# A streaming encoder step on one core: later values and merged matmuls of two heads, the spatial product from high and low parts, free weight splits behind the due ones

## The chip, the cores and the metric

The kernel runs on one core of a Trainium2 chip. The metric is the device time of one execution in microseconds, as the median of the runs shown. One more execution is recorded by the hardware profiler; its views are what the prediction reads. Beside the engines TensorE (PE, its weight loads PEld), VectorE (DVE), ScalarE (ACT), GpSimd (POOL) and SyncE (SP) work the DMA queues that SP, ACT and POOL issue to.

## The reference

384 rows of activations (256 of a prompt, 8 times 16 of running streams) go through two layers, all in float32.

```python
# layer 0: RMSNorm, one projection to q, k, v, gate of 8 forgetting heads and 8 stick-breaking heads
s = einsum('bqhd,bkhd->bhqk', q, k) * ATTN_SCALE + (Fq - Fk)     # forgetting: F is a running sum of log gates
o = einsum('bhqk,bkhd->bqhd', softmax(where(causal, s, -inf)), v)
a = where(before, exp(log_sigmoid(z) + after), 0.0)              # stick-breaking: sums of log_sigmoid(-z)
hp = hp + concatenate([fo * silu(fz), so * silu(sz)]) @ w_out0
# layer 1: RMSNorm, projection to u, v, z (4096 each); v is layer-normalised
mixed = einsum('gts,bnsgc->bntgc', tril(w_sp), v_in_16_groups_of_256) + b_sp
hp = hp + (u * mixed * silu(z)) @ w_out1
y = rmsnorm(hp, final_g)
```

Running streams also attend to 128 cached rows each, so that keys and values of the caches are read. The new keys, values, log gates and the normalised v are outputs too.

## The kernel before, in words

**Projections.** The 384 rows are three blocks of 128 (`NT`). The transposed activations are the stationary operand, in a high and a low part (`his`, `los`); a weight tile of 128x512 is loaded by SP into `raw` (5 buffers), ScalarE rounds it to `whi` (L84) and VectorE takes the rest, `wlo` (L86); four buffers of each. `products` (L93) makes three matmuls for each weight tile and row block: high by high, high by low, low by high (L100 to L102). `dense_nat` (L105) goes through the tiles in pairs, 18 matmuls a pair, and adds up in three banks. A projection of 512 columns in 16 tiles is 144 matmuls.

**The attention of layer 0** works in four groups of four heads (`quad`, L466): groups 0 and 1 are forgetting heads, 2 and 3 stick-breaking ones. Each group projects k, q, z and v (group 0: k, v, q, z). `head` (L601) is a generator: each `next` or `send` issues one stage. `scores` (L478) makes the score matmuls in plain float32 (L626 to L632) and the softmax or its stick-breaking counterpart of two heads; the weights `pr` go to DRAM by ScalarE's queue (L667) and come back in another order by GpSimd's (L492, four loads for two heads) so that VectorE's transpose within blocks (L670) completes the transposition into `PT`. `attended` (L497) then makes the products with the values (L678 to L686), multiplies them with the gate `gz` (L689, L691), and writes them to DRAM (L504). When all four heads are through, `blocks` (L391) loads them back, and `mix_split` (L587) transposes and splits them for the output projection.

**What sets the order.** `at(g, what, kp, f)` fills a table: work `f` is issued in the projection `what` of group `g`, ahead of its weight tile `kp`. `places` (L511) has the four places of a group: scores of heads 0 and 1, scores of 2 and 3, values of 0 and 1, values of 2 and 3; `(what == "k")` means the next group. The framework's scheduler then orders each engine's instructions by its own estimate of time; `tc.issue_after(x)` holds an instruction behind `x`. Each engine's queue runs strictly in the order so made. `gains(1)` (L162, called at L356) transposes the second layer's norm gains on TensorE and copies them out of their bank (L165); the forget sums (L358 to L373) follow it there.

**Layer 1.** v is projected, normalised in place in `vt` (`normalise`, L780: L787, L788), and each of 8 chunks of 512 columns then goes as follows: the spatial weights of two groups are loaded, transposed and masked (`spatial_weights`, L829); z and u are projected to `gate`; the spatial product (L862) is a plain float32 matmul of 128x256 for each row block and group, 48 in all; gate times product (L865) is transposed by VectorE and 16 small DMAs (`turn`, L119), split into high and low parts (L872, L873), and multiplied with `w_out1` after chunks 2, 4 and 6 (`out1`, L821) and 7. Scratch has two buffers of `gate` and of `wT`, and one of `trn`.

**The last part.** The last four k-tiles of `w_out1` are kept back (`KL = 4`): their 16 weight tiles are split ahead by `last_split` (L888), some between the tiles of the last `out1` ("due" splits), the rest free; `last` (L913) then finishes one row block after the other (L921 to L923, with pieces of 512 and of 256 columns), and `norm` writes the result.

Of the kernel before, what the change touches and what calls it, by code (L numbers as in the profile page):

```python
# [8 lines left out]
F32 = mybir.dt.float32  # L9
# [28 lines left out]
def tile_hybrid_step(  # L38
# [54 lines left out]
    def products(out, his, los, ws, kp, tbs, first, last):  # L93
# [9 lines left out]
        return mm  # L103

    def dense_nat(w, k0, c0, his, los, nk=None, between=None, out=None, ks=None):  # L105


        nk = nk or len(his)
        out = out or [dbank() for _ in range(NT)]
        for kp in range(0, nk, 2) if ks is None else ks:  # L110
            behind = ()
            if between and kp in between:
                with tc.issue_after(splits[-1]), tc.issue_after(highs[-1]):
                    behind = between[kp]() or ()
            ws = [wunit(w[(k0 + k) * P:(k0 + k + 1) * P, c0:c0 + 512], 1, 512, behind=behind) for k in (kp, kp + 1)]
            products(out, his, los, ws, kp, range(NT), 0, nk - 1)
        return out
# [39 lines left out]
    with ExitStack() as l0:  # L157
# [185 lines left out]
        def forget(o):  # L343
# [11 lines left out]
            yield  # L355
            gains(1)  # L356
            b3 = bank()
# [108 lines left out]
        def quad(g):  # L466
# [11 lines left out]
            def scores(pair):  # L478

                for hh in pair:  # L480
                    hs = slice(hh * P, hh * P + P)
                    own[hh] = head(g, h0 + hh, own["k"][:, hh], lambda hs=hs: own["v"][:, :, hs], own["q"][:, hh],
                                   keys_of[4 * g + hh], lambda n=4 * g + hh: values_of[n], lambda hs=hs: own["z"][:, :, hs])
                wd = own[pair] = dram.tile([2, 6, P, P], F32, name=nm("wd"))
                for hh in pair[::-1]:
                    next(own[hh])
                for _ in range(2):
                    for j, hh in enumerate(pair):
                        own[hh].send(wd[j])
                blk = own["blk", pair] = slot(F32).rearrange("p (j x) -> p j x", j=2)  # L490
                for j in range(4):
                    G.dma_start(blk[32 * j:32 * j + 32].rearrange("p j (a d) -> p (j a) d", d=32),  # L492
                                wd[:, :, :, 32 * j:32 * j + 32].rearrange("j x (a p) d -> p (j x a) d", p=32))
# [20 lines left out]
            for i, (what, kp) in enumerate(places):  # L514
                at(g + (what == "k"), what, kp, lambda i=i: (scores, attended)[i // 2](((0, 1), (2, 3))[i % 2]))
            at(g + 1, "q", (12, 8, 8, 8)[g], lambda: mix_split())

# [83 lines left out]
        def head(g, h, kT, values, qT, kc, vc, gate):  # L601
# [67 lines left out]
            PT = lp.tile([P, 2 * T], F32, tag="PT", name=nm("PT"))  # L669
            V.transpose(out=PT, in_=blk)  # L670
            yield
            PD = PT[:, T:]
# [89 lines left out]
    with ExitStack() as l1:  # L762
# [47 lines left out]

        ghi, glo, fgs = [], [], []
        KL = 4

        def wlast(c, k):
# [14 lines left out]
        def spatial_weights(g):  # L829
# [9 lines left out]
            return wT  # L839

        for c in range(8):
            wTs = [spatial_weights(2 * c + i) for i in range(2)]
            o = dense_nat(w_in1, 0, 2 * CW + c * 512, hh_, hl_)
            gate = lp.tile([P, NT, 512], F32, tag="gate", name=nm("gate"))
            for tb in range(NT):
# [6 lines left out]
            else:  # L852

                for j in range(2):
                    fg = slot(F32)[:, :1024]
                    G.dma_start(fg, final_g[j * 1024:(j + 1) * 1024].partition_broadcast(P))
                    fgs.append(fg)
            for tb in range(NT):
                m = bank()
                for i in range(2):  # L860
                    cs = slice(c * 512 + i * 256, c * 512 + i * 256 + 256)
                    PE.matmul(m[:, i * 256:(i + 1) * 256], lhsT=wTs[i][:, tb // 2, :], rhs=vt[:, tb, cs], start=True, stop=True)  # L862
                for i in range(2):
# [6 lines left out]
            for k in range(4):  # L870
                h3 = hi[:, k, :].rearrange("p (t q) -> p t q", q=P)
                S.activation(h3, gk_[:, k], AF.Copy)  # L872
                V.tensor_tensor(out=lo[:, k, :].rearrange("p (t q) -> p t q", q=P), in0=gk_[:, k], in1=f32(h3), op=ALU.subtract)  # L873
# [5 lines left out]
        order = [(c, k) for c in range(4) for k in range(KL)]  # L879
        x = lp.tile([P, NT, 512], F32, tag="gate", name="early")  # L880
        aside = {ck: x[:, j, :] for j, ck in enumerate(order[:3])}
        for ck, raw in aside.items():
            G.dma_start(raw, wlast(*ck))
        wl = {}
# [28 lines left out]
        def last(tb, i):  # L913
# [11 lines left out]
            V.tensor_tensor(out=ht, in0=o, in1=ht, op=ALU.add)  # L925
            sq2 = lp.tile([P, NT, 512], F32, tag="gate", name=nm("sq2"))[:, 0, :]
            S.activation(sq2[:, :n], ht, AF.Square, accum_out=ssq2[:, tb, i:i + 1])
# [64 lines left out]
```

## Time and profile before

| what | value |
|---|---|
| runs | 1812.33, 1812.5, 1813.67 us; median 1812.5 |
| the profiled execution | 1815.39 us |
| its span, first to last instruction | 1813.7 us |
| granted TensorE clock, mean | 0.995 |
| busy: TensorE, VectorE, ScalarE, GpSimd | 99%, 51%, 39%, 20% |
| matmuls recorded | 8575 (a float32 one counts as two) |
| DMA | 307.63 MB, mean 170 GB/s |

The sum of a change is made against the profiled execution's own 1815.39 us and then carried over to the median, which is 2.9 us lower. Rows of the timeline give start, length, engine, line, operation and tiles; in brackets stands the idle time before it and what ended it. A row of waits gives the total, how often, and the longest. Lengths of matmuls overlap, so TensorE's pace is read from one start to the next.

### The profile page before, as it was taken

The numbers are of one execution on the slowest core, as the hardware profiler recorded it, in microseconds if no ns is written. First come the engines' busy times: TensorE is split into PE (matmuls) and PEld (weight loads), VectorE is DVE, ScalarE is ACT, GpSimd is POOL, SyncE is SP. The second block draws the span as 40 slices with busy tenths as digits, with TensorE's granted clock in tenths as the row PEclk, the third lists the DMA queues.
The fourth block names the chain that finished last, engine by engine and source line by source line (L and its number), as shares of the span: only waits on it lengthen the run. The fifth ranks groups of instructions, "written<-read, shape, count | busy, mean of one in ns | idle before, by whom it ended". The sixth has DMA issues, their size and how long they took to land. (4 is left out here: it accounts for less than half of the span.)

```text
span 1813.7 us, 24384 instructions
## 1 busy us (share of the span) xinstructions
PE 1788.8 (99%) x8575; PEld 1483.8 (82%) x8575; DVE 924.2 (51%) x1538; ACT 710.2 (39%) x1261; POOL 369.9 (20%) x544
## 2 busy tenths in 40 slices
PE   9999799999999999999999999999999999999998
PEld 8988588888888888888888888888888888888887
DVE  6337356458448455543433544554544563455366
ACT  5435236337337344433333333333333333333334
POOL 1515524313312202200300120320130210220020
PEclk9999899999999999999999999999999999999999
DMA  6868778878876877644444444454544554555553
GB/s 195 233 179 212 201 216 216 251 196 206 238 207 179 241 204 207 189 128 128 135 129 131 138 137 146 148 146 130 157 143 128 146 154 128 145 146 150 164 145 117
DMA packets 185771, 307.63 MB, mean 170 GB/s; under 512 B 22904, under 2 KB 63152, under 8 KB 185648
## 3 DMA queue, kind: packets, MB, share of 16 engines
q1 hardware_dynamic: 127696, 225.37, 42.1%
q0 software_dynamic: 25072, 63.53, 14.1%
q10 hardware_dynamic: 32880, 17.18, 3.2%
q8 instruction: 67, 1.10, 0.3%
q14 instruction: 56, 0.46, 0.1%
HBM read 269.23 MB, written 30.47 MB: 165 GB/s over the span
## 5 line engine op out<-in xcount | busy, mean ns | idle before, releaser
L86 DVE TENSOR_TENSOR wlo<-raw,whi 128x512 fp32r<-128x512 f32 x784 | 538.0, 695 | 745.1 <-ACT whi L84 744.9
L101 PE MATMUL d<-wlo,slot 128*128 128x512 f32 x2349 | 916.6, 391 | 0.2
L102 PE MATMUL d<-whi,slot 128*128 128x512 f32 x2349 | 912.0, 389 | 0.0
L84 ACT ACTIVATE whi<-raw 128x512 fp32r<-128x512 f32 x784 | 493.4, 631 | 944.9 <-PE d L102 889.3
L100 PE MATMUL d<-whi,slot 128*128 128x512 f32 x2349 | 822.9, 391 | 0.0
L100 PEld LDWEIGHTS d<-whi,slot 128*128 128x128 f32 x2349 | 440.9, 188 | 94.3 <-ACT whi L84 1.6
L101 PEld LDWEIGHTS d<-wlo,slot 128*128 128x128 f32 x2349 | 441.0, 188 | 91.7 <-DVE wlo L86 1.0
L102 PEld LDWEIGHTS d<-whi,slot 128*128 128x128 f32 x2349 | 441.0, 188 | 91.5
L126 POOL DMA_DIRECT2D gTt<-trn x128 | 78.0, 618 | 446.0 <-issue 263.9
L396 POOL DMA_DIRECT2D slot<-d x48 | 44.1, 924 | 145.9 <-DVE wlo L86 53.6
L492 POOL DMA_DIRECT2D slot<-wd x32 | 29.4, 924 | 103.4 <-DMA wd<-pr 34.6
L833 POOL DMA_DIRECT2D wr<-in_w_sp_dram x64 | 34.9, 553 | 26.2 <-DVE wT L837 25.1
L826 DVE TENSOR_TENSOR slot<-d,slot 128x512 f32<-128x512 f32 x48 | 32.0, 686 | 12.4 <-PE d L102 12.4
L783 POOL DMA_DIRECT2D slot<-in_sgu_ln_g_dram x8 | 4.5, 567 | 135.5 <-PE d L102 135.5
L455 POOL DMA_DIRECT2D kcache<-in_cache_sb_k_dram x32 | 24.9, 786 | 32.4 <-DVE KT L621 32.4
L455 POOL DMA_DIRECT2D kcache<-in_cache_fox_k_dram x32 | 25.0, 789 | 23.4 <-DVE KT L621 22.2
L709 POOL DMA_DIRECT2D blk<-h1d x12 | 11.0, 919 | 70.7 <-DMA h1d<-slot 60.4
L799 POOL DMA_DIRECT2D bcol<-in_b_sp_dram x1 | 1.2, 1176 | 116.1 <-DVE w L798 116.1
L862 PE MATMUL a<-vt,wT 128*128 128x256 f32 x96 | 24.5, 380 | 0.0
L777 POOL TENSOR_SCALAR rsv<-mvr 128x3 f32<-128x3 f32 x1 | 0.5, 540 | 113.0 <-DVE mvr L776 113.0
L774 DVE BATCH_NORM_STATS2 stats<-vt 128x6 f32<-128x512 f32 x24 | 16.3, 690 | 11.4 <-ACT vt L773 11.4
L849 DVE SCALAR_TENSOR_TENSOR gate<-d,rstd,gate 128x512 f32<-128x512 f32 x24 | 17.4, 748 | 7.3 <-PE d L102 7.3
(239 smaller groups left out, 1201.3 us busy)
## 6 DMA issues: line engine op xcount, KB each, us to landing
raw<-in_w_in_dram SPq DMA_DIRECT2D x640, 256.0 KB, 2.8
raw<-in_w_out_dram SPq DMA_DIRECT2D x189, 256.0 KB, 3.4
slot<-d POOLq DMA_DIRECT2D x48, 192.0 KB, 6.2
d<-slot ACTq DMA_DIRECT2D x24, 256.0 KB, 3.9
wd<-pr ACTq DMA_DIRECT2D x16, 384.0 KB, 5.8
slot<-wd POOLq DMA_DIRECT2D x32, 192.0 KB, 5.3
gTt<-trn POOLq DMA_DIRECT2D x128, 48.0 KB, 3.5
kcache<-in_cache_fox_k_dram POOLq DMA_DIRECT2D x32, 128.0 KB, 5.8
```

What stands on the lines that cost most here:

```text
L84: highs.append(S.activation(hi, raw, AF.Copy).ins)
L86: splits.append(V.tensor_tensor(out=lo, in0=raw, in1=f32(hi), op=ALU.subtract).ins)
L100: PE.matmul(o, lhsT=his[k][:, t], rhs=hi[:, 0, :], start=(k == first), stop=False)
L101: PE.matmul(o, lhsT=his[k][:, t], rhs=lo[:, 0, :], start=False, stop=False)
L102: mm = PE.matmul(o, lhsT=los[k][:, t], rhs=hi[:, 0, :], start=False, stop=(k == last))
L126: G.dma_start(dst[32 * j:32 * j + 32, :, 32 * a:32 * a + 32], trn[32 * a:32 * a + 32, :, 32 * j:32 * j + 32])
L396: r = G.dma_start(blk[32 * j:32 * j + 32].rearrange("p h (a d) -> p (h a) d", d=32), d[:, :, 32 * j:32 * j + 32].rearrange("h (a p) d -> p ...
L455: G.dma_start(k[32 * j:32 * j + 32].rearrange("p (b d) -> p b d", d=32), (c_fox_k, c_sb_k)[n // 8][:, :, n % 8, 32 * j:32 * j + 32].rearra ...
L492: G.dma_start(blk[32 * j:32 * j + 32].rearrange("p j (a d) -> p (j a) d", d=32), wd[:, :, :, 32 * j:32 * j + 32].rearrange("j x (a p) d -> ...
L826: evicted = V.tensor_tensor(out=h1[c][:, tb, :], in0=o[tb], in1=h1[c][:, tb, :], op=ALU.add)
L833: G.dma_start(wr[js, 0, :].rearrange("p (a s) -> p a s", s=32), w_sp[g, :, js].rearrange("(a p) s -> p a s", p=32))
L862: PE.matmul(m[:, i * 256:(i + 1) * 256], lhsT=wTs[i][:, tb // 2, :], rhs=vt[:, tb, cs], start=True, stop=True)
```

## The change

The diff, cut to its core (renamed lines and the helper's reuse of buffers follow from it):

```diff
+            last_product[:] = [products(out, his, los, ws, kp, range(NT), 0, nk - 1).ins]
...
-            gains(1)
             b3 = bank()
...
             V.tensor_copy(Fnat, b4[:, :24].rearrange("p (t h) -> p t h", h=8))
+            gains(1)
...
-                for _ in range(2):
-                    for j, hh in enumerate(pair):
-                        own[hh].send(wd[j])
+                with tc.issue_after(last_product[0]):
+                    for hh in pair:
+                        next(own[hh])
+                for j, hh in enumerate(pair):
+                    own[hh].send(wd[j])
...
-                for j, hh in ((1, pair[1]), (0, pair[0])):
-                    own[hh].send(own["blk", pair][:, j, :])
-                for hh in pair:
-                    next(own[hh])
+                turned = [own[hh].send(own["blk", pair][:, j, :]) for j, hh in ((1, pair[1]), (0, pair[0]))]
+                with tc.issue_after(turned[0].ins), tc.issue_after(turned[1].ins):
+                    for hh in pair:
+                        next(own[hh])
...
-            places = ((("z", 12), ("k", 2), ("k", 8), ("k", 12)), (("z", 12), ("v", 2), ("k", 2), ("k", 8)))[g > 0]
+            places = (((0, "z", 12), (1, "k", 2), (1, "k", 12), (1, "q", 4)), ((0, "z", 12), (0, "v", 2), (1, "k", 2), (1, "k", 8)))[g > 0]
...
-            at(g + 1, "q", (12, 8, 8, 8)[g], lambda: mix_split())
+            at(g + 1, *(("z", 4) if g == 0 else ("q", 8)), lambda: mix_split())
...
-            wT = lp.tile([P, 2, P], F32, tag="wT", name=nm("wT"))
+            wT = lp.tile([P, 2, P], F32, tag="wT", bufs=1, name=nm("wT"))
...
+            wh = lp.tile([P, 2, P], F32R, tag="wTh", name=nm("wTh"))
+            wl = lp.tile([P, 2, P], F32R, tag="wTl", name=nm("wTl"))
+            split(wh, wl, wT)
+            return wh, wl
+
+        def split_values(c):
+
+            vh = lp.tile([P, NT * 4, P], F32R, tag="trn", bufs=1, name=nm("vh")).rearrange("p (t x) q -> p t (x q)", t=NT)
+            vl = lp.tile([P, NT, 512], F32R, tag="vl", bufs=1, name=nm("vl"))
+            for tb in range(NT):
+                split(vh[:, tb, :], vl[:, tb, :], vt[:, tb, c * 512:c * 512 + 512])
+            return vh, vl
...
-                    PE.matmul(m[:, i * 256:(i + 1) * 256], lhsT=wTs[i][:, tb // 2, :], rhs=vt[:, tb, cs], start=True, stop=True)
+                    PE.matmul(o, lhsT=wh[:, tb // 2, :], rhs=vh[:, tb, cs], start=True, stop=False)
+                    PE.matmul(o, lhsT=wh[:, tb // 2, :], rhs=vl[:, tb, cs], start=False, stop=False)
+                    PE.matmul(o, lhsT=wl[:, tb // 2, :], rhs=vh[:, tb, cs], start=False, stop=True)
...
+            if c < 7:
+                vhl = split_values(c + 1)
...
-        while len(order) > 9:
-            last_split()
+        with tc.issue_after(splits[-1]), tc.issue_after(highs[-1]), tc.issue_after(turned.ins):
+            while len(order) > 9:
+                last_split()
```

In words: in group 0 the values of heads 0 and 1 move from weight tile 8 of the next group's k to tile 12, those of heads 2 and 3 from tile 12 of that k to tile 4 of its q, and mixing from tile 12 of q to tile 4 of z. In all groups the score matmuls of two heads are held behind the last projection matmul issued, and the value products of two heads behind both transposes, so that they stand together. `gains(1)` comes after the forget sums. In layer 1 the spatial weights and the normalised values are split into high and low parts, and three matmuls of fp32r take the place of one of float32; `gate` and `wT` get one buffer instead of two, and `vh` shares the buffer of `trn`. Three raw tiles of the last part go to a slot of their own instead of `gate`'s second buffer. At the end the four free splits that stood between the due ones are held behind the last due split and the transposed gate.

The order shows three places. First TensorE, around the values of heads 2 and 3 of group 0 (`d` are the banks of a projection, `whi` its weight tiles with their numbers, `PT` the transposed softmax weights). Before, with 138 projection matmuls since the same heads' last score row:

```order
L102 MATMUL d_397_2157<-whi_410_2198,slot_13_130 128x512
L678 MATMUL a_377_2033<-vnat_104_611,PT_376_2031 32x128 x4
L682 MATMUL a_377_2033<-vcache_361_1965,PT_376_2031 32x128 x8
L678 MATMUL a_378_2046<-vnat_104_611,PT_375_2029 32x128 x4
L682 MATMUL a_378_2046<-vcache_362_1967,PT_375_2029 32x128 x8
```

and now, with 214 of them:

```order
L100 MATMUL d_392_2106<-whi_428_2288,slot_16_133 128x512
L681 MATMUL a_407_2171<-vnat_104_611,PT_406_2169 32x128 x4
L685 MATMUL a_407_2171<-vcache_373_2025,PT_406_2169 32x128 x8
L681 MATMUL a_408_2184<-vnat_104_611,PT_405_2167 32x128 x4
L685 MATMUL a_408_2184<-vcache_374_2027,PT_405_2167 32x128 x8
```

The piece itself is the same; it stands 76 projection matmuls later, in q instead of k.

Second VectorE, at the two transposes that this piece needs. Before:

```order
L86 TENSOR_TENSOR wlo_408_2194<-raw_406_2190,whi_407_2192 128x512
L86 TENSOR_TENSOR wlo_411_2200<-raw_409_2196,whi_410_2198 128x512
L670 STREAM_TRANSPOSE PT_375_2029<-slot_336_1816 128x768
L670 STREAM_TRANSPOSE PT_376_2031<-slot_336_1816 128x768
L689 SCALAR_TENSOR_TENSOR gz_300_1679<-a_377_2033,st_328_1780,gz_300_1679 128x128 x2
```

and now:

```order
L86 TENSOR_TENSOR wlo_426_2284<-raw_424_2280,whi_425_2282 128x512
L86 TENSOR_TENSOR wlo_429_2290<-raw_427_2286,whi_428_2288 128x512
L674 STREAM_TRANSPOSE PT_405_2167<-slot_336_1816 128x768
L674 STREAM_TRANSPOSE PT_406_2169<-slot_336_1816 128x768
L86 TENSOR_TENSOR wlo_432_2314<-raw_430_2310,whi_431_2312 128x512
L86 TENSOR_TENSOR wlo_435_2320<-raw_433_2316,whi_434_2318 128x512
L86 TENSOR_TENSOR wlo_438_2344<-raw_436_2340,whi_437_2342 128x512
L692 SCALAR_TENSOR_TENSOR gz_300_1679<-a_407_2171,st_328_1780,gz_300_1679 128x128 x2
```

The transposes moved behind six more weight splits, and three further splits now stand between them and the multiplication with the gate.

Third VectorE in layer 1, where the transposed gate of chunk 0 is split (`gTt`), and the values of chunk 1 now too (`vl`). Before:

```order
L86 TENSOR_TENSOR wlo_1991_9819<-raw_1989_9815,whi_1990_9817 128x512
L873 TENSOR_TENSOR slot_1936_9569<-gTt_1933_9549,slot_1935_9568 128x384 x4
L86 TENSOR_TENSOR wlo_1998_9850<-raw_1996_9846,whi_1997_9848 128x512
L86 TENSOR_TENSOR wlo_2001_9856<-raw_1999_9852,whi_2000_9854 128x512
L86 TENSOR_TENSOR wlo_2004_9880<-raw_2002_9876,whi_2003_9878 128x512
L86 TENSOR_TENSOR wlo_2007_9886<-raw_2005_9882,whi_2006_9884 128x512
L787 SCALAR_TENSOR_TENSOR vt_6963<-vt_6963,mvr_6965,slot_2044_10089 128x512 x3
```

and now:

```order
L86 TENSOR_TENSOR wlo_2003_9863<-raw_2001_9859,whi_2002_9861 128x512
L898 TENSOR_TENSOR slot_1942_9597<-gTt_1939_9577,slot_1941_9596 128x384 x4
L91 TENSOR_TENSOR vl_1944_9607<-vt_6963,vh_1943_9606 128x512 x2
L790 SCALAR_TENSOR_TENSOR vt_6963<-vt_6963,mvr_6965,slot_2056_10133 128x512 x3
L91 TENSOR_TENSOR vl_1944_9607<-vt_6963,vh_1943_9606 128x512
L86 TENSOR_TENSOR wlo_2010_9894<-raw_2008_9890,whi_2009_9892 128x512
```

Three splits of values and the normalising that stood four weight splits later now stand between two weight splits.

More of the change, by code (lines that the diff above doesn't have):

```diff
@@ L508, in attended @@
                     mixed.append(blocks(own["d"])[0])
-            places = ((("z", 12), ("k", 2), ("k", 8), ("k", 12)), (("z", 12), ("v", 2), ("k", 2), ("k", 8)))[g > 0]
+            places = (((0, "z", 12), (1, "k", 2), (1, "k", 12), (1, "q", 4)), ((0, "z", 12), (0, "v", 2), (1, "k", 2), (1, "k", 8)))[g > 0]
             at(g, "q", 2 if g == 0 else 14, lambda: turned("k"))
             at(g, "z", 12, lambda: turned("q"))
-            for i, (what, kp) in enumerate(places):
-                at(g + (what == "k"), what, kp, lambda i=i: (scores, attended)[i // 2](((0, 1), (2, 3))[i % 2]))
-            at(g + 1, "q", (12, 8, 8, 8)[g], lambda: mix_split())
+            for i, (later, what, kp) in enumerate(places):
+                at(g + later, what, kp, lambda i=i: (scores, attended)[i // 2](((0, 1), (2, 3))[i % 2]))
+            at(g + 1, *(("z", 4) if g == 0 else ("q", 8)), lambda: mix_split())
             def evict(o, dst, scale, n=512):
@@ L809, in tile_hybrid_step @@
         G.affine_select(out=btri, in_=btri, pattern=[[-16, 8], [-1, 16]], compare_op=ALU.is_ge, fill=0.0, base=0, channel_multiplier=1)
-        ghi, glo, fgs = [], [], []
+        ghi, glo, fgs, aside = [], [], [], {}
         KL = 4
+        order = [(c, k) for c in range(4) for k in range(KL)]
         def wlast(c, k):
@@ L843, in tile_hybrid_step @@
             o = dense_nat(w_in1, 0, 2 * CW + c * 512, hh_, hl_)
-            gate = lp.tile([P, NT, 512], F32, tag="gate", name=nm("gate"))
+            gate = lp.tile([P, NT, 512], F32, tag="gate", bufs=1, name=nm("gate"))
             for tb in range(NT):
@@ L857, in tile_hybrid_step @@
                     fgs.append(fg)
+                x = slot(F32).rearrange("p (j c) -> p j c", j=3)
+                for j, ck in enumerate(order[:3]):
+                    aside[ck] = x[:, j, :]
+                    G.dma_start(x[:, j, :], wlast(*ck))
             for tb in range(NT):
@@ L875, in tile_hybrid_step @@
             glo.append(lo)
+            if c < 7:
+                vhl = split_values(c + 1)
             if c in (2, 4, 6):
                 out1((c - 2) * 4, 8)
[L879 to L883, printed above, removed]
         wl = {}
```

15 lines of the change are left out of this document (8 added, 7 removed).

## The prediction

> **What bounds the kernel now.** I read the page's first two parts first, to see which engine has no slack and where it stops.
>
> ```profile
> span 1813.7 us, 24384 instructions
> ...
> PE 1788.8 (99%) x8575; PEld 1483.8 (82%) x8575; DVE 924.2 (51%) x1538; ACT 710.2 (39%) x1261; POOL 369.9 (20%) x544
> ...
> PE   9999799999999999999999999999999999999998
> ...
> PEclk9999899999999999999999999999999999999999
> ```
>
> TensorE is busy in 99% of the span. A single slice, the fifth, drops to 7, and the clock drops with it. Elsewhere the time is the sum of the starts of matmuls, so a change pays only if it shortens what stands in TensorE's row or removes a stop there. Next came the list of TensorE's waits.
>
> ```profile
> PE a L678 <- DVE PT L670: 13.5, 1, 13.5
> PE a L373 <- DVE gT L165: 1.3, 1, 1.3
> PE a L196 <- DVE ones L132: 1.1, 1, 1.1
> PE a L219 <- DMA slot<-in_x_sample_dram: 0.3, 1, 0.3
> ```
>
> One wait of 13.5 us matters: the product with the values (L678) of heads 2 and 3 of the first group waits until VectorE has transposed the weights (L670). The timeline of TensorE prices it, beside the same product of the second group (320.67 on), which waits for nothing. Columns: start, length, instruction.
>
> ```profile
> 195.63 0.39 PE L102 MATMUL d<-whi,slot 128*128 128x512 f32 x1
> 209.53 0.65 PE L678 MATMUL a<-vnat,PT 128*32 128x128 f32 x8 [13.51 <-DVE PT L670]
> 214.32 0.48 PE L100 MATMUL d<-whi,slot 128*128 128x512 f32 x1
> 320.67 0.39 PE L101 MATMUL d<-wlo,slot 128*128 128x512 f32 x1
> 320.90 0.39 PE L102 MATMUL d<-whi,slot 128*128 128x512 f32 x1
> 324.03 0.47 PE L100 MATMUL d<-whi,slot 128*128 128x512 f32 x1
> ```
>
> Projection matmuls start every 0.23 us (320.67, 320.90; I count 0.227). From the last projection before the piece to the first behind it, it takes 18.69 us at 195.63 and 3.13 at 320.90: 15.56 us more, of which 13.5 are the wait. The rest is the clock, in the windows (the last three numbers are granted clock, DMA share and GB/s):
>
> ```profile
> 196.00:200.00 4.00, 0.02 (x1) 0.00 (x0) 0.00 (x0) 0.24 (x1) 0.00 (x0) 1.00 0.91 269
> 200.00:208.00 8.00, 0.00 (x0) 0.00 (x0) 0.36 (x1) 0.00 (x0) 6.41 (x8) 0.51 0.55 146
> 208.00:212.00 4.00, 2.47 (x48) 2.17 (x48) 1.48 (x2) 0.00 (x0) 0.63 (x1) 0.50 0.08 16
> ```
>
> The clock is still full through the first 4 us of idleness and is halved after it, so the piece itself runs at half clock. Who is late is read from ScalarE's, GpSimd's and VectorE's timelines and the page's table of DMA issues (last number: median us from issue to landing).
>
> ```profile
> 185.53 0.38 ACTq L667 DMA_DIRECT2D wd<-pr  x1
> 200.46 3.70 POOL L492 DMA_DIRECT2D slot<-wd  x4 [9.53 <-DMA wd<-pr]
> 207.64 1.84 DVE L670 STREAM_TRANSPOSE PT<-slot 128x768 f32<-128x768 f32 x2 [12.41 <-DMA slot<-wd]
> wd<-pr ACTq DMA_DIRECT2D x16, 384.0 KB, 5.8
> slot<-wd POOLq DMA_DIRECT2D x32, 192.0 KB, 5.3
> ```
>
> The softmax weights leave at 185.53, GpSimd gets to load them back at 200.46 (a trip of some 14 us where the median is 5.8), and VectorE starts at 207.64. It ends at 209.48. That is a chain of transfers; TensorE merely asked too early.
>
> **The change part by part.** *Later values.* The orders of before and after put 138 projection matmuls between the scores of heads 2 and 3 and their values, and now 214. The 76 more take 76 x 0.227 = 17.25 us, so TensorE asks at 195.63 + 17.25 = 212.9. If the chain ends as it did, at 209.5, the wait is gone with 3.4 us to spare, and 15.56 us with it. But the chain ran while TensorE stood and the weight stream had ebbed (DMA share 0.55). With the median of 5.3 for the last of the four loads, issued at 203.2, the transposes end at 203.2 + 5.3 + 1.8 = 210.3. If the softmax weights also leave 3 us later (their last part now stands on VectorE behind the products of heads 0 and 1), TensorE waits 0.4 us. Ends: nothing and 3 us; I take 0.3, near the first end, since both nearest rows leave it uncovered only when they add up. VectorE has the two transposes six weight splits later than before; blocked there, it holds back the next splits, which TensorE needs only behind the value piece (3 us). *Mixing* moves along with the values, still 144 projections behind them, and on VectorE eight weight splits behind the last product as in the last group, where nothing waits: nothing.
>
> *gains(1)* moves behind the forget sums. L373 waited for a bank that L165 empties; the bank it takes now was emptied long before. The 1.3 us go. They could come back as one wait for another bank: 0 to 1.3, I take the whole gain.
>
> *Merged matmuls.* The first pair of each group already had its scores in one piece (268.63 to 271.71), the second had them in five pieces with 19 projections from the first row to the last (279.78 to 287.00).
>
> ```profile
> 268.63 0.39 PE L102 MATMUL d<-whi,slot 128*128 128x512 f32 x1
> 271.71 0.50 PE L100 MATMUL d<-whi,slot 128*128 128x512 f32 x1
> 279.78 0.39 PE L102 MATMUL d<-whi,slot 128*128 128x512 f32 x1
> 287.00 0.50 PE L100 MATMUL d<-whi,slot 128*128 128x512 f32 x1
> ```
>
> One piece: 3.08 - 0.23 = 2.85. Five pieces: 7.22 - 19 x 0.227 = 2.91. Four groups save 4 x 0.06 = 0.2 us; the merged values of heads 0 and 1 I count at nothing. Merging costs nothing else: both heads' transposes are done long before.
>
> *Spatial product.* Now 48 float32 matmuls of 256 columns; then 144 of the high and low parts. The price of the first is read where four stand together, that of the second from the last part of the kernel, which has such matmuls, each with its own weight load.
>
> ```profile
> 1071.77 0.84 PE L100 MATMUL d<-whi,slot 128*128 128x512 f32 x3
> 1072.45 1.89 PE L862 MATMUL a<-vt,wT 128*128 128x256 f32 x8
> 1073.98 0.58 PE L101 MATMUL d<-wlo,slot 128*128 128x512 f32 x1
> 1074.40 0.40 PE L102 MATMUL d<-whi,slot 128*128 128x512 f32 x1
> ...
> 1788.35 0.28 PE L921 MATMUL d<-slot,slot 128*128 128x256 f32 x1
> 1788.46 0.28 PE L922 MATMUL d<-slot,slot 128*128 128x256 f32 x1
> 1788.47 0.19 PEld L923 LDWEIGHTS d<-slot,slot 128*128 128x128 f32 x1
> 1789.18 0.28 PE L922 MATMUL d<-slot,slot 128*128 128x256 f32 x1
> ```
>
> Without the four, L102 would start at 1072.45 + 0.23 = 1072.68 instead of 1074.40: 1.72 us, 0.43 each with the return to the projections; 48 x 0.43 = 20.6 us. From 1788.35 to 1789.18 seven matmuls start, 0.119 apart; 144 x 0.119 = 17.1. Gain 3.5 us. The Trainium skill (FP8 and Floating Point Precision, section TensorE Precision Notes) says that true FP32 takes four passes through the array; three reduced passes would then cost 0.75 x 0.43, the 48 products 15.5 us and the gain 5.1. The trace's 3 x 0.119 = 0.36 against 0.43 decides for 3.5.
>
> The splits for it are new: in each of eight chunks three of 128x512 and two of 128x256 on ScalarE and VectorE.
>
> ```profile
> L91 DVE TENSOR_TENSOR wlo<-raw,whi 128x512 fp32r<-128x512 f32 x16 | 10.9, 689 | 17.8 <-ACT whi L90 17.8
> 1095.38 1.95 DVE L873 TENSOR_TENSOR slot<-gTt,slot 128x384 fp32r<-128x384 f32 x4
> 1104.11 2.07 DVE L787 SCALAR_TENSOR_TENSOR vt<-vt,mvr,slot 128x512 f32<-128x512 f32 x3
> 1010.00:1690.00 680.00, 679.79 (x2999) 562.29 (x2998) 332.03 (x536) 228.66 (x373) 108.14 (x185) 1.00 0.50 145
> 1760.00:1790.00 30.00, 30.00 (x140) 25.04 (x139) 22.86 (x38) 14.85 (x31) 0.00 (x0) 1.00 0.37 114
> ```
>
> On VectorE that is 3 x 0.69 + 2 x 0.45 (between 0.34, half of the large one, and 0.69) = 3.0 us a chunk, 24 in all, beside 332 busy of 680. What hides it is VectorE's idle half, and the four buffers of each weight half. Worst is the first chunk, where the order puts 1.95 + 3 x 0.69 + 2.07 = 6.1 us between two weight splits. A pair of weights feeds 18 matmuls, 4.1 us; the buffers give two pairs less the two splits (1.4): 6.8 us. 6.1 plus the next split, 0.7, just reaches it. Ends: 0 and 4 us (half a microsecond in each chunk); I take 0.5, since seven chunks are less dense. TensorE was full in this part before, so freeing VectorE gains nothing.
>
> *Free splits behind the due ones* at the end: TensorE is busy 30.0 of 30.0 us there, so nothing is to be won. The first product of the last part needs one of the splits moved back; the transposed gate's four (1.95) and this one (0.69) fit in the 6.8 us of cover. Ends 0 and 2; I take 0.
>
> **Sum.** 15.6 + 1.3 + 0.2 + 3.5 - 0.3 - 0.5 = 19.8 us. The profiled execution took 1815.39 us with a span of 1813.7, so it becomes 1795.6; the median of the three runs, 1812.5, becomes 1792.7.
>
> **The rivals.** *A, part of the wait stays.* For it: DMA share 0.91 at 196 and a weight trip of 14 us; the weight stream no longer ebbs. Against: 3.4 us of spare. A wait of 3 to 8 us, the longer ones at half clock afterwards: 1796 to 1801. 14%.
>
> *B, the wait moves whole.* If the trip is delayed as much as the request, by the weight transfers that now go on, 15.6 us stand in place of the 0.3: 1808.0. Against it: up to the request, GpSimd's order issues the same transfers ahead of it as before. 6%.
>
> *C, weight loads bind the narrow products.* 144 loads of 0.19 us are 27.4 us where 17.1 are forecast: 10.3 us more, 1803.0. The row at 1788.47 speaks against it: the load lasts 0.19, yet matmuls start every 0.119. [...] 5%.
>
> *D, slower: VectorE becomes the bound in layer 1.* If none of the new splits is hidden, because each stands in its row between weight splits that TensorE already waits for, 8 x 3.0 = 24 us come in place of the 0.5: 1816.2. It decides against the change from 20.3 / 8 = 2.5 us a chunk. For it: only the burst at the first chunk. Against: 51% idle. 4%.
>
> **How the numbers follow.** The forecast has 71%, by itself 1790 to 1796 (lower end: no losses, 0.8, and 1.9 for a better price of the products; upper: 3 us of wait). With most of A the range is 1789.5 to 1799. A measurement of this kernel can tell about 0.2%, 3.6 us. Forecast, A, B and C are faster by more (96%); D gives 3 slower and 1 same; for a mishap in an unknown place I move 1 from faster to same: 0.95, 0.02, 0.03.
>
> **What would show it.** TensorE's waits without L678 (its new line L681) and L373, the clock 0.99 or more in the fifth slice, value pieces of about 3.1 us each. The spatial matmuls 0.12 us apart, with no stop over 0.5 us around VectorE's splits in layer 1. A wait at L681 of over 3 us, or gaps of 1 us or more in each chunk, would prove the sum wrong.

## The result, and the profile after

The kernel after takes 1795.61 us in the median of four runs (1793.76 to 1795.94), the one before 1813.09 beside it. The ratio is 0.9902, with a 95% interval of 0.9887 to 0.9916: 17.5 us less, where 19.8 were forecast. A second comparison, among the experiments, gave 1794.29 and 0.9893 (0.9878 to 0.9908), 18.9 us less.

The page of after, its span, busy times and slices:

```profile
span 1794.2 us, 24567 instructions
PE 1782.1 (99%) x8623; PEld 1480.1 (82%) x8623; DVE 946.6 (53%) x1578; ACT 729.0 (41%) x1301; POOL 369.9 (21%) x544
PE   9999999999999999999999999999999999999998
PEclk9999999999999999999999999999999999999999
```

The hole in the fifth slice is gone, and the clock's dip with it. The list of TensorE's waits in after (us in total, times, longest):

```profile
PE d L101 <- DVE wlo L86: 1.7, 3, 1.3
PE a L198 <- DVE ones L134: 1.1, 1, 1.1
PE a L886 <- DVE vl L91: 0.5, 3, 0.2
PE d L253 <- DVE slot L228: 0.4, 1, 0.4
```

The waits of 13.5 us at the values and of 1.3 at L373 are no longer there. The first row is new: 1.3 us for the low part of a weight tile, which no step of the prediction had. It is followed up below. First the piece that had waited, in TensorE's timeline of after:

```profile
209.71 0.39 PE L100 MATMUL d<-whi,slot 128*128 128x512 f32 x1
210.02 0.43 PE L681 MATMUL a<-vnat,PT 128*32 128x128 f32 x8
...
212.69 0.39 PE L689 MATMUL a<-vnat,PT 128*128 128x128 f32 x2
212.83 0.47 PE L101 MATMUL d<-wlo,slot 128*128 128x512 f32 x1
```

From projection to projection it now lasts 212.83 - 209.71 = 3.12 us, as the piece of the second group did. VectorE and GpSimd show why it no longer waits:

```profile
205.73 1.84 DVE L674 STREAM_TRANSPOSE PT<-slot 128x768 f32<-128x768 f32 x2 [0.85 <-DMA slot<-wd]
```

```profile
194.37 3.68 POOL L496 DMA_DIRECT2D slot<-wd  x4 [7.22 <-issue]
```

GpSimd loads the weights at 194.37 and VectorE has transposed them by 207.57, 2.5 us before TensorE asks (3.4 were forecast).

Now the new stop, first on TensorE and then on VectorE, both from after's timelines:

```profile
236.31 0.39 PE L100 MATMUL d<-whi,slot 128*128 128x512 f32 x1
237.99 0.50 PE L101 MATMUL d<-wlo,slot 128*128 128x512 f32 x1 [1.30 <-DVE wlo L86]
```

```profile
229.92 0.69 DVE L86 TENSOR_TENSOR wlo<-raw,whi 128x512 fp32r<-128x512 f32 x1 [2.13 <-ACT whi L84]
235.58 1.78 DVE L594 STREAM_TRANSPOSE vnat<-slot 128x1536 f32<-128x1536 f32 x1 [4.97 <-DMA slot<-d]
237.29 1.25 DVE L86 TENSOR_TENSOR wlo<-raw,whi 128x512 fp32r<-128x512 f32 x2
```

VectorE stands 4.97 us in front of the transpose for mixing (L594), whose data is not yet loaded. Behind it in its row wait the next weight splits, and TensorE waits for the first of them. The two starts on TensorE lie 1.68 us apart where 0.23 is usual.

To compare profiles stage by stage I count projection matmuls (L100 to L102), the first one as number 0: both kernels have 7191 of them, so number n starts at the same point of the work. Against the first profile of before, after is 1.52 us earlier at the first one, and from there to the last gains 17.93 us more: 1.56 up to number 135 (L373), 15.63 from number 441 to 656 (the values of heads 2 and 3), 1.57 lost from 750 to 760 (the mixing), some 0.3 by merging in four groups, and 2.08 from number 2300 to the last, which is layer 1. What lies behind the last projection takes 41.9 us in both.

### The profile page after: what moved, and what is told of

Its sections match the earlier page's. It is cut to its first block, busy times and chain, and to the rows that moved or that the text cites. A ratio compares the mean times of both kernels' runs of the same rounds, so it can differ in the third digit from the quotient of the medians.

```text
span 1794.2 us, 24567 instructions
## 1 busy us (share of the span) xinstructions
PE 1782.1 (99%) x8623; PEld 1480.1 (82%) x8623; DVE 946.6 (53%) x1578; ACT 729.0 (41%) x1301; POOL 369.9 (21%) x544
## 4 chain that ended last, share of the span: by engine, by line
PE 95%; DMA 2%; issue 1%; DVE 1%; POOL 1%; ACT 0%; POOLq 0%; DVEq 0%; ACTq 0%
PE d L100 29%; PE d L102 29%; PE d L101 29%; DMA slot<-in_sgu_ln_b_dram 1%; PE a L101 1%; PE a L100 1%; PE a L102 1%; DMA d<-gz 0%; PE a L636 0%; DMA slot<-d 0%; PE a L630 0%; PE a L886 0%; PE d L426 0%; PE a L685 0%; PE d L944 0%
## 5 line engine op out<-in xcount | busy, mean ns | idle before, releaser
L102 PE MATMUL d<-whi,slot 128*128 128x512 f32 x2349 | 911.5, 389 | 0.0
L100 PE MATMUL d<-whi,slot 128*128 128x512 f32 x2349 | 822.4, 390 | 0.0
L100 PEld LDWEIGHTS d<-whi,slot 128*128 128x128 f32 x2349 | 440.6, 188 | 93.9 <-issue 0.8
L102 PEld LDWEIGHTS d<-whi,slot 128*128 128x128 f32 x2349 | 440.9, 188 | 91.1
L830 DVE TENSOR_TENSOR slot<-d,slot 128x512 f32<-128x512 f32 x48 | 32.4, 689 | 13.8 <-PE d L102 13.8
L457 POOL DMA_DIRECT2D kcache<-in_cache_fox_k_dram x32 | 25.0, 787 | 22.1 <-DVE KT L625 20.9
L777 DVE BATCH_NORM_STATS2 stats<-vt 128x6 f32<-128x512 f32 x24 | 16.2, 689 | 11.6 <-ACT vt L776 11.6
L862 ACT ACTIVATE gate<-d,rstd 128x512 f32<-128x512 f32 x24 | 16.5, 689 | 11.2 <-PE d L102 11.1
```

The source lines that it names most:

```text
L100: PE.matmul(o, lhsT=his[k][:, t], rhs=hi[:, 0, :], start=(k == first), stop=False)
L102: mm = PE.matmul(o, lhsT=los[k][:, t], rhs=hi[:, 0, :], start=False, stop=(k == last))
L457: G.dma_start(k[32 * j:32 * j + 32].rearrange("p (b d) -> p b d", d=32), (c_fox_k, c_sb_k)[n // 8][:, :, n % 8, 32 * j:32 * j + 32].rearra ...
L830: evicted = V.tensor_tensor(out=h1[c][:, tb, :], in0=o[tb], in1=h1[c][:, tb, :], op=ALU.add)
```

## The experiments

**The kernel before once more**, without an edit.

> The kernel before, profiled a second time. In its first profile the first projection matmul starts 10.13 us into the span, after the change at 8.61: 1.52 us that no part of the change accounts for. Theory (the start varies from execution to execution): another start, between 8 and 11 us, and the same waits as in the first profile, 13 to 14 us at L678 and 1.3 at L373, total 1811 to 1816. Rival (the start belongs to the order of the kernel before): 10.1 us again, within 0.2, and the change then owns 1.5 us that the sum doesn't contain.

TensorE's waits in this second profile of before:

```profile
PE a L678 <- DVE PT L670: 13.2, 1, 13.2
PE a L196 <- DVE ones L132: 1.1, 1, 1.1
PE a L219 <- DMA slot<-in_x_sample_dram: 0.6, 1, 0.6
PE a L373 <- DVE gT L165: 0.5, 1, 0.5
```

The profiled execution took 1815.26 us. The wait at the values stands as it was; the one at L373 is 0.5 in place of 1.3. The first projection starts at 10.84. Over all thirteen profiles of this study it starts between 8.28 and 8.79 or between 9.98 and 10.84: 10.13 and 8.71 in programs with layer 0 as before, 8.61 and 10.36 in programs whose first 50 us are those of after. The 1.52 us of the start are therefore no part of the change, as the theory had it.

**The later places alone**, on the kernel before: the two lines of the table, with the loop that reads it.

```diff
-            places = ((("z", 12), ("k", 2), ("k", 8), ("k", 12)), (("z", 12), ("v", 2), ("k", 2), ("k", 8)))[g > 0]
+            places = (((0, "z", 12), (1, "k", 2), (1, "k", 12), (1, "q", 4)), ((0, "z", 12), (0, "v", 2), (1, "k", 2), (1, "k", 8)))[g > 0]
...
-            at(g + 1, "q", (12, 8, 8, 8)[g], lambda: mix_split())
+            at(g + 1, *(("z", 4) if g == 0 else ("q", 8)), lambda: mix_split())
```

> The kernel before with the later places for values and mixing alone. Theory (this place is worth 15.6 us, and the mixing behind it now costs 1.6): a wait of 13.5 us gone at L678, a new one of 1 to 2 us for a weight split behind the mixing transpose L590, and 14 us (13.3 to 15) less up to the 819th projection matmul: 1799 at the kernel before's median of 1813.1. Rival one (part of the gain needs the merged matmuls, which hold the value products behind both transposes): 11 us or less. Rival two (the new wait at the mixing comes from the merged matmuls, not from the places): 15.6 us and no such wait.

TensorE's largest wait, and VectorE's row at the mixing (L590 in this kernel):

```profile
PE d L101 <- DVE wlo L86: 3.0, 1, 3.0
```

```profile
240.21 1.78 DVE L590 STREAM_TRANSPOSE vnat<-slot 128x1536 f32<-128x1536 f32 x1 [6.71 <-DMA slot<-d]
```

The values gain 15.63 us, as much as in after, without the merged matmuls: rival one falls. So does rival two, since the stop at the mixing is here too. It is 3.30 us (by starts), twice that of after, so the program is 12.35 us ahead at projection 819, where I had expected 13.3 to 15. One execution took 1802.43, where 1799 was expected.

**The values of heads 2 and 3 put back**, in the kernel after; the mixing stays in its place in the table.

```diff
-            places = (((0, "z", 12), (1, "k", 2), (1, "k", 12), (1, "q", 4)), ((0, "z", 12), (0, "v", 2), (1, "k", 2), (1, "k", 8)))[g > 0]
+            places = (((0, "z", 12), (1, "k", 2), (1, "k", 12), (1, "k", 14)), ((0, "z", 12), (0, "v", 2), (1, "k", 2), (1, "k", 8)))[g > 0]
```

> The changed kernel with the values of heads 2 and 3 of group 0 alone put back to 138 projection matmuls behind their scores; mixing stays eight splits behind. Theory (the chain of transfers, not TensorE's request, sets when the transposes end, and the full DMA behind the request is what makes the mixing late): TensorE waits 12 to 15 us at L681, at half clock behind it, the wait of 1.3 us behind the mixing transpose is gone: 13 to 15 us more, 1809 to 1811. Rival (the changed place of heads 0 and 1 or the merged order already shortens the chain): a wait under 8 us, 1804 or less.

TensorE's waits in this kernel:

```profile
PE a L681 <- DVE PT L674: 12.2, 1, 12.2
PE a L198 <- DVE ones L134: 1.1, 1, 1.1
PE a L886 <- DVE vl L91: 0.4, 2, 0.2
```

12.2 us come back in one place (14.3 with the slower clock behind it), and the stop at the mixing is gone: 1809.24. For the values the theory held: the chain of transfers sets the time, whenever TensorE asks. For the mixing the expectation had one thing wrong: its transpose stands sixteen weight splits behind the last product of the values here and not eight, since only the values moved back. So the missing stop is no proof by itself. But the eighth split ends at 226.93, and the last load for the mixing lands at 227.95 in the trace: 1.0 us of idling at the old distance, close to the 0.63 of before, where TensorE did not stop.

What stretches the chain to the mixing is seen where the stored heads (d from gz) go out ahead of it. The windows of after around that place (the last three numbers are granted clock, DMA share, GB/s), and the issues of 213 to 229 us with their median time to landing:

```profile
212.00:220.00 8.00, 8.00 (x42) 6.75 (x41) 5.37 (x10) 1.90 (x3) 3.77 (x5) 1.00 1.03 325
220.00:228.00 8.00, 8.00 (x37) 6.63 (x36) 2.76 (x4) 4.29 (x7) 2.82 (x4) 1.00 0.97 309
```

```profile
slot<-d POOLq DMA_DIRECT2D x4, 192.0 KB, 7.0
d<-gz POOLq DMA_DIRECT2D x2, 192.0 KB, 9.1
```

The same in this experiment, the windows and the issue of 211 to 214 us:

```profile
204.00:212.00 8.00, 5.27 (x62) 4.65 (x63) 2.71 (x6) 0.00 (x0) 1.82 (x2) 0.55 0.26 72
212.00:220.00 8.00, 8.00 (x37) 6.59 (x36) 3.54 (x7) 2.62 (x5) 4.43 (x6) 1.00 0.61 197
```

```profile
d<-gz POOLq DMA_DIRECT2D x2, 192.0 KB, 3.5
```

Around TensorE's wait the weight stream ebbs (share 0.26, then 0.61), and the stores land 3.5 us after issue. Where TensorE never stands, the share is 1.03 and the same stores need 9.1. The queues show whose transfers these are, first in before (215 to 219.3 us), then in after (214.5 to 224.7), each while the stores are under way. Packets, MB and share of the DMA engines; q1 is the queue that carries the weights, 225 of 308 MB over the whole kernel, and q0 the one of GpSimd:

```profile
q0 software_dynamic: 278, 0.91, 58.8%
d<-gz POOLq DMA_DIRECT2D x2, 192.0 KB, 3.5
```

```profile
q0 software_dynamic: 703, 2.30, 61.2%
q1 hardware_dynamic: 716, 1.32, 36.8%
```

In before no weights move beside the stores, in after they take 36.8%. From the issue of the first store to the landing of the mixing's last load, the traces show 15.0 to 16.2 us in the four profiles in which TensorE stood at the values, and 19.7 to 21.6 in the nine others. The wait that the change removed had kept the way clear for the mixing. How much of the longer trip is the weights, and how much GpSimd's own loads beside them, is not separated.

**The kernel after again, and the mixing later.** These two and the last two below (scale and shift) were timed together, each in four runs, beside seven of before (median 1813.17).

> The changed kernel once more, on the chip of the versions it is compared with. Theory: 1795.6 within 1; the wait of 1.3 us for a weight split behind the mixing transpose (L594) of group 0 is there again, since full DMA stretches every such trip. Rival (a chance of that one execution): no wait there.

```diff
-            at(g + 1, *(("z", 4) if g == 0 else ("q", 8)), lambda: mix_split())
+            at(g + 1, *(("z", 8) if g == 0 else ("q", 8)), lambda: mix_split())
```

> The changed kernel with the mixing of group 0 at tile 8 of z instead of tile 4: its transpose stands three weight splits later on VectorE. Theory (VectorE stood 4.97 us in front of it while weight splits waited behind it): the wait of 1.57 us is gone, nothing new comes: 1794.0. Rival (the transfers come later too, pushed by the weights that go on): a wait of 1 us or more at another split, 1795.6. Rival on the other side (the mixed parts are then late for something behind): slower than 1795.6.

VectorE at the mixing, in the kernel after again, then with the mixing later:

```profile
233.48 1.78 DVE L594 STREAM_TRANSPOSE vnat<-slot 128x1536 f32<-128x1536 f32 x1 [2.75 <-DMA slot<-d]
```

```profile
237.04 1.78 DVE L594 STREAM_TRANSPOSE vnat<-slot 128x1536 f32<-128x1536 f32 x1 [1.79 <-DMA slot<-d]
```

After again took 1794.29 (1793.59 to 1795.94), and its profile has no stop at the mixing at all: my expectation fell, the rival (a chance of that execution) held. With the mixing later it took 1794.42 (1794.09 to 1795.50), ratio 0.9894 (0.9877 to 0.9910): no measurable difference. The stop is absent there as well, though the transpose could not start before 237.04, later than in after (235.58), where TensorE stopped: the three further weight splits cover a late chain. The median gains nothing from it; after again had no stop in its profile to lose. The profiles of all kernels that mix at the place of after, with the values behind 214 projections, give the rule. VectorE's idle time ahead of the transpose, the excess on TensorE by its starts, and the difference:

| kernel | idle us | stop us | difference |
|---|---|---|---|
| later places alone | 6.71 | 3.30 | 3.41 |
| two spatial products | 5.71 | 2.30 | 3.41 |
| three small parts undone | 4.98 | 1.57 | 3.41 |
| after | 4.97 | 1.56 | 3.41 |
| split of the values twice | 2.85 | 0 | |
| after again | 2.75 | 0 | |
| scale and shift elsewhere | 2.74 | 0 | |

There is 3.4 us of cover at this place. What exceeds it, TensorE waits, one for one, and the transpose stands behind the 69th weight split on VectorE in all seven. Whether it exceeds hangs on when the transfers land in that execution, four times in seven here.

The traces show where these executions part. GpSimd loads k back (its first four slot<-d of this stretch) ahead of the mixing, and those loads wait for three stores of k from ScalarE's queue. The third store in after and in after again, issued at 190.91 and 191.03, with the time to landing:

```profile
d<-slot ACTq DMA_DIRECT2D x1, 256.0 KB, 15.4
```

```profile
d<-slot ACTq DMA_DIRECT2D x1, 256.0 KB, 7.5
```

In the four executions that stop it takes 15.3 to 17.1 us, in the three others 7.4, 7.5 and 13.4. Where it is late, everything behind it is: GpSimd begins to load k at 206.85 in after and at 202.00 in after again, sends the second of the stored heads at 215.79 and 214.52, and has the mixing's data at 235.50 and 233.40. That is an order seen in seven profiles; no edit tried it.

**The spatial product alone**, all else as before (places, gains(1), merging, free splits).

> The changed layer 1 alone: spatial product from high and low parts with its buffers, everything else (places, gains(1), merging, free splits) as before. Theory: layer 1 is 2.1 us shorter, as in the changed kernel (3.2 by the matmuls' own starts, 1.1 given back in longer stops), layer 0 is unchanged, with 13 to 14 us of wait at the values: 1811. Rival (the record's price of the splits, 0.5): 3.0 us. Rival (four passes for float32, three for the parts): 5 us.

It took 1810.95. For layer 1 I take the time from projection 2300 to the last:

| kernel | layer 1, us |
|---|---|
| before, its two profiles | 1130.92, 1130.45 |
| later places alone | 1130.47 |
| after, its two profiles | 1128.84, 1128.68 |
| mixing later | 1128.94 |
| values of heads 2 and 3 back | 1127.67 |
| spatial product alone | 1127.39 |
| two spatial products | 1122.75 |
| split of the values twice | 1132.77 |
| scale and shift elsewhere | 1128.84 |
| that and mixing later | 1129.65 |
| three small parts undone | 1129.10 |

So the spatial product gains 3.5 us in this execution against the first profile of before (3.1 against the second), and 2.1 in after. On each engine the order of layer 1 is the same in after and in the kernel with the values put back, and yet they are 1.2 us apart. The difference lies in chunks 3, 5 and 7. Starts that come over 0.06 us later than the usual spacing (0.227 us behind a projection, 0.119 behind a spatial product), from projection 3936 on, add up to 2.4 us in after, 1.4 with the values put back and 1.0 with the spatial product alone. One such place in after, on VectorE and then on TensorE:

```profile
1650.22 0.75 DVE L791 SCALAR_TENSOR_TENSOR vt<-vt,rsv,slot 128x512 f32<-128x512 f32 x1 [0.62 <-DMA slot<-in_sgu_ln_b_dram]
...
1653.42 0.69 DVE L91 TENSOR_TENSOR vl<-vt,vh 128x512 fp32r<-128x512 f32 x1
1654.02 0.69 DVE L830 TENSOR_TENSOR slot<-d,slot 128x512 f32<-128x512 f32 x1
```

```profile
1653.71 0.28 PE L885 MATMUL a<-vh,wTh 128*128 128x256 f32 x1
1654.16 0.38 PE L886 MATMUL a<-vl,wTh 128*128 128x256 f32 x1 [0.17 <-DVE vl L91]
1654.38 0.28 PE L887 MATMUL a<-vh,wTl 128*128 128x256 f32 x1
1654.50 0.28 PE L885 MATMUL a<-vh,wTh 128*128 128x256 f32 x1
```

Normalising waits for its shift vector, the split of the values stands behind it, and the product behind that; the later products stand 0.12 us apart, as forecast. I had taken one profile's 2.1 us for the part's worth; it is 1.5 to 3.5, and the 3.0 on record lies inside.

**Two spatial products instead of three**

```diff
-                    PE.matmul(o, lhsT=wh[:, tb // 2, :], rhs=vl[:, tb, cs], start=False, stop=False)
-                    PE.matmul(o, lhsT=wl[:, tb // 2, :], rhs=vh[:, tb, cs], start=False, stop=True)
+                    PE.matmul(o, lhsT=wh[:, tb // 2, :], rhs=vl[:, tb, cs], start=False, stop=True)
```

> The changed kernel without the third of the three spatial products (low part of the weights times high part of the values): 48 matmuls of 256 columns less; this part of the computation is left out. Theory (each costs the time between two starts, 0.119 us): 5.7 us less in layer 1, 1789.9. Rival (the weight load of 0.19 us binds): 9.0 us less. Rival (a pass costs a quarter of a float32 product's 0.43 us): 5.2 us less. Rival (the products stand where TensorE waits for VectorE anyway): under 4 us less.

Layer 1 is 6.09 us shorter than in after and 5.93 shorter than in after again: 0.124 to 0.127 for each of 48 products. That is little more than their own starts (5.7), and their loads of 0.19 us don't bind (9.0 would have gone). The Trainium skill (FP8 and Floating Point Precision, section TensorE Precision Notes) counts four passes for float32; as an estimate from that, a pass would cost a quarter of the 0.43 us, 0.107. The trace doesn't agree with that as a price: the product costs 0.119 to 0.127, and 0.43 is 3.4 to 3.6 of them. This execution took 1790.35, a stop of 2.30 us at the mixing included.

**The values split twice**

```diff
-            for tb in range(NT):
-                split(vh[:, tb, :], vl[:, tb, :], vt[:, tb, c * 512:c * 512 + 512])
+            for _ in range(2):
+                for tb in range(NT):
+                    split(vh[:, tb, :], vl[:, tb, :], vt[:, tb, c * 512:c * 512 + 512])
```

> The changed kernel with the values' split done twice in each chunk: 24 more tiles of 128x512 on ScalarE and on VectorE, 0.69 us each on VectorE, 16.5 us in all. Theory (VectorE has room in layer 1 except around the products of chunks 3, 5 and 7, where the split ends last): in these three some 2 us each, elsewhere nothing: 3 to 8 us more in all, 1799 to 1804. Rival (VectorE bounds all of layer 1): 16 us or more, 1812. Rival (all is hidden, and the stops come from the loads of the normalisation alone): under 1 us more.

The first row of TensorE's waits in this kernel:

```profile
PE d L100 <- DVE slot L830: 2.7, 3, 0.9
```

Layer 1 is 3.9 us longer, for 16.5 us of VectorE's time: most of it is hidden. One execution took 1798.19. What is not stands in chunks 3, 5 and 7, where TensorE now waits for banks that VectorE adds to the residual too late. The rivals fall: VectorE doesn't bound layer 1, and its work isn't free either.

**The three small parts undone**

```diff
+            gains(1)
             b3 = bank()
...
-                with tc.issue_after(last_product[0]):
...
-                with tc.issue_after(turned[0].ins), tc.issue_after(turned[1].ins):
...
-        with tc.issue_after(splits[-1]), tc.issue_after(highs[-1]), tc.issue_after(turned.ins):
-            while len(order) > 9:
-                last_split()
+        while len(order) > 9:
+            last_split()
```

> The changed kernel with its three small parts undone: gains(1) back ahead of the forget sums, score and value matmuls no longer held together, the free splits of the last part back between the due ones. The three stand far apart, so the profile prices each. Theory: 1.3 to 1.6 us of wait at L373 comes back, the merging gives 0.06 us a group (0.2 in all), the free splits nothing (under 0.2): 1797.4. Rival for the merging (it keeps value products away from late transposes): a wait of over 1 us at one of the value pieces. Rival for the free splits: over 0.5 us behind the first product of the last part.

TensorE's waits in this kernel:

```profile
PE d L101 <- DVE wlo L86: 1.5, 2, 1.3
PE a L198 <- DVE ones L134: 1.1, 1, 1.1
PE a L375 <- DVE gT L167: 0.9, 1, 0.9
```

Against after, 1.27 us come back by projection 135 (the wait for gains(1), L375 here), as forecast, and 0.32 through the four groups, where 0.2 were. No value product waits, so the rival for the merging falls. The free splits are worth 0.3 where I had said nothing: in the last output product one split is late, as this kernel's timeline of TensorE shows.

```profile
1745.60 0.39 PE L100 MATMUL d<-whi,slot 128*128 128x512 f32 x1
1745.98 0.50 PE L101 MATMUL d<-wlo,slot 128*128 128x512 f32 x1
1746.32 0.40 PE L102 MATMUL d<-whi,slot 128*128 128x512 f32 x1
```

0.38 and 0.34 stand where 0.23 is usual. The same gap is in the kernel with the spatial product alone and in none of the three profiles with layer 1 as before: the new splits make the free ones late, and their new place mends that. One execution took 1797.52.

**Scale and shift in another buffer**, meant to free the normalising in chunks 3, 5 and 7 from waiting for a slot.

```diff
-            lg = slot(F32)[:, :1024].rearrange("p (a c) -> p a c", a=2)
+            lg = lp.tile([P, NT * 4, P], F32, tag="gTt", bufs=1, name=nm("lg"))[:, :8, :].rearrange("p (a x) q -> p a (x q)", a=2)
```

> The changed kernel with the scale and shift of the normalisation of layer 1 loaded into the buffer of the transposed gate instead of a slot: in chunks 3, 5 and 7 their loads no longer wait for a slot that an output product frees, so that normalising and splitting the values stand earlier and apart from the other work of VectorE. Theory (2.4 us of stops in layer 1 come from this crowd): 1 to 2.4 us less, 1793.2 to 1794.6. Rival (the crowd comes from the transposed gate's split and the weights alone): no change, 1795.6. Rival (a single shared buffer makes the next chunk's load wait for the gate): 1 us or more slower.

> The changed kernel with both edits: mixing at tile 8 of z, and scale and shift in the buffer of the transposed gate. Theory: the sum of the two, 2.6 to 4 us less than the changed kernel, 1791.6 to 1793. Rival: if one of the two only moves its stop, half of that or nothing.

TensorE's waits with the buffer changed alone:

```profile
PE a L198 <- DVE ones L134: 1.1, 1, 1.1
PE d L100 <- DVE slot L830: 0.9, 2, 0.6
```

The waits for the split of the values (L886) have gone, and waits for the residual's additions (L830) stand in their place. Layer 1 takes 1128.84 us, as in after, and 1129.65 with the mixing later as well. The medians are 1794.73 (1794.51 to 1795.73; ratio 0.9895, 0.9880 to 0.9910) and, with both edits, 1795.39 (1794.14 to 1796.83; 0.9898, 0.9883 to 0.9913). My theory, that the crowd around the products could be thinned, falls for this edit: it moves the stop. Nor did the edit free the normalising: VectorE now idles 12.2 us in all ahead of it (L790, seven times, up to 4.5) until its scale has landed in the shared buffer, where after has 2.6. What thinning the crowd would bring is therefore not shown. Apart from the kernel with two products, which leaves a part of the computation out, no version here is measurably faster than the kernel after.

## Why the prediction was right, and where not

*The values.* 15.6 us forecast, 15.63 found, with the places alone as well (15.2 against the second profile of before). The residual wait of 0.3 did not come: rivals A and B fell. That the chain ends earlier than TensorE asks, by 2.5 us in place of 3.4, was the step at risk, and it held by luck in part. The way back through DRAM was longer than forecast, 8.4 us for the last of the four loads in place of 5.3, and the way out shorter, 9.9 in place of the 14.2 that the prediction kept; together 22.1, against 21.6 in before.

*The mixing* is the step that failed. The prediction let it move along "still 144 projections behind" the values "where nothing waits: nothing". It had counted instructions, and the distance was indeed kept; but the trip that lies within that distance was one of the kernel before, made after TensorE had stood, with no weights moving beside the stores. With the weight stream going on, the stores take 9.1 us in place of 3.5, the transpose comes late, and TensorE stops by what exceeds 3.4 us: by 1.6 to 3.3 in four executions of seven, by nothing in three. For the values the prediction had weighed the stronger traffic; for the next chain behind them it had not.

*gains(1)*: 1.3 forecast, 1.56 found against the first profile of before. The whole wait went, but it is itself 0.5 to 1.3 from one execution to another.

*Merging*: 0.2 forecast, 0.3 found.

*Spatial product*: 3.5 less 0.5 for bursts on VectorE. The products' own starts cost what was forecast (0.119 to 0.127 each). The term for the stops was too small: 1.0 to 2.5 us in place of 0.5. They were put at the first chunk, as the worst; they came in chunks 3, 5 and 7, where the shift vector lands late. The net is 1.5 to 3.5 in these profiles. Rivals C and D fell with the two experiments on them.

*Free splits*: nothing forecast, 0.3 found, and only beside the new layer 1.

*The sum.* In after again, where the mixing doesn't stop, the part from the first projection to the last gains 19.5 us, against 19.8 on record. That nearness is luck in part: the values and gains(1) bring 0.6 more than their terms, layer 1 0.8 less, and against the second profile of before it is 18.7. In the first profile of after the gain is 17.9, with the stop of 1.6. The medians are 17.5 and 18.9 us apart, and the forecast of 1792.7 was 2.9 and 1.6 us too low. A stop of 0 to 3.3 at the mixing and a layer 1 that gains 2 rather than 3 are of that size.

What stays open: why the third store of k lands 7 us after its issue in one execution and 15 in another. The late chain to the mixing follows it in the profiles, but no experiment moved that store.

## What to carry to other kernels

A stop on the bounding engine also idles the queues that feed it. Whoever removes it must price every chain of transfers behind it again, at the landing times of full traffic, not of the profile with the stop in it; the distance in instructions says nothing about that. And where one profile gives a part's worth in microseconds, a second profile of the same kernel shows how many of them are chance.

## What the runs showed of the hardware

The same stores of 192 KB needed 3.5 us at a DMA share of 0.26 to 0.61, with no weights moving beside them in before, and 9.1 at about 1.0, with the weights' queue at 36.8%. The start of the first projection falls into two groups (8.28 to 8.79 and 9.98 to 10.84), with members of both among programs that are alike up to there. Of the 0.43 us that a float32 product of 256 columns costs in the row, some lies behind it: in before the second projection after such a group starts 0.42 us behind the first, in place of 0.23.
